# Weight loads of a hybrid decoder layer issued from ScalarE's DMA queue instead of SP's

## Chip, cores and metric

One Trainium2 chip, one NeuronCore of it. The metric is the device time of one execution in microseconds, the median of several runs. The kernel before takes 1884.48 us.

## The reference

One decoder layer on 2048 tokens and 16 meta tokens, model width 1024, all in float32. One input projection makes six groups of 1024 columns: q, k, v, a gate for the attention, the input and the gate of a linear recurrence (LRU). Eight heads of stick-breaking attention and eight blocks of a gated recurrence read the same normalised rows; both results are gated, normalised and go through one output projection.

```python
def hybrid_layer(h, ...):
    u = rmsnorm(h, pre_g)
    p = u @ w_in
    q, k, v, g_att, x_lru, g_lru = jnp.split(p, ...)
    att = rmsnorm(stick_breaking_attention(q, k, v), att_out_g) * jax.nn.silu(g_att)
    lru = rglru_branch(x_lru, conv_w, conv_b, gate_a_w, gate_a_b, gate_x_w, gate_x_b, lru_lambda)
    lru = rmsnorm(lru, lru_out_g) * jax.nn.silu(g_lru)
    y = jnp.concatenate([att, lru], axis=-1) @ w_out
    return h + rmsnorm(y, post_g)

def stick_breaking_attention(q, k, v):
    ...
        z = jnp.einsum('bhqd,bhkd->bhqk', qi, kh) * scale
        log_beta = jax.nn.log_sigmoid(z)
        log_1m = jnp.where(mask, log_beta - z, 0.0)
        suffix = lax.cumsum(log_1m, axis=3, reverse=True) - log_1m
        w = jnp.where(mask, jnp.exp(log_beta + suffix), 0.0)
        return jnp.einsum('bhqk,bhkd->bhqd', w, vh)
```

## The kernel before

Every product keeps float32 accuracy by splitting each operand into a high and a low half and multiplying three times (high-high, high-low, low-high).

**Projection.** The normalised rows lie in SBUF, transposed, as uH and uL. The 48 column blocks of w_in (128 columns each) are loaded one by one, 512 KB each, into a raw buffer (`wraw`, one of it; three of the first four go to spare rows and show as `lrow`). `load_w` is a generator: its first step issues the load (line 143), the next ones find the block's largest value (VectorE reduce at line 146, a small TensorE product at 152), scale it and split it into wH (ScalarE, line 161) and wL (VectorE, line 163). The end of wL frees the raw buffer. wH and wL have three buffers each; one comes free when the last chunk of its block has gone through TensorE (line 174, 24 matmuls a chunk). The chunk's result is evicted by ScalarE (line 792 for q and k, 841 for v, 888 for the gates, 341 for the LRU input).

**Attention.** For each head and 128 queries a segment of up to 1040 keys goes: scores on TensorE (line 219), sigmoid on ScalarE (223), a mask on GpSimd (228), a running product on VectorE (233), the split into two halves by ScalarE (245) and VectorE (251), a DMA transpose on the SP queue (256) that gives wT, and the product with v on TensorE (270). There are 208 segments.

**LRU.** For each of eight blocks the weights of its two gates (128 KB) are loaded by `lru_gates_w` (line 326) into one buffer `graw`; the next two lines split them into gH (ScalarE, 327) and gL (VectorE, 328). Behind that come a convolution (VectorE, lines 357 and 360), the gates' products (379, 380) and a recurrence (414).

**Order.** A planner (`Plan`, `weave`) runs when the program is built. It keeps an estimated free time for each engine, and emits an instruction when its inputs are ready by that estimate. For a load it reckons 0.6 us of SP and 4.5 us until the data are there (`LD`), at the start 0.5, 1.46 and 2.0 (`LDX`); `weight` emits the load and plans the reduce at that time. The order of TensorE, ScalarE and VectorE stays as emitted:

```python
    with tc.manual_schedule(engines={mybir.EngineType.PE, mybir.EngineType.Activation, mybir.EngineType.DVE}):
        start()
        weave()
```

The scheduler underneath orders SP and GpSimd itself, and may issue a load on SP as soon as its buffer is free. `weight` is called by `loader`, as soon as both a pair of wH/wL buffers and the raw buffer are free in the plan. `mix_start` calls `lru_gates_w` when a block's first half of LRU input is there, and reckons `LD` for it on ScalarE.

Of the kernel before, what the change touches and what calls it, by code (L numbers as in the profile page):

```python
# [70 lines left out]
def hybrid_layer(nc, tc, I, out):  # L71
    import contextlib
    act, dve, pool, pe, sp = nc.scalar, nc.vector, nc.gpsimd, nc.tensor, nc.sync
# [57 lines left out]
    def load_w(col, home=None, raw=None):  # L131


        if raw is None:
            raw = wp.tile([P, KT, P], F32, name="wraw", bufs=1)
        else:
            raw = raw[:, :D].rearrange("p (k c) -> p k c", k=KT)
        if home is None:
            wH = wp.tile([P, KT, P], F16, name="wH", bufs=3)
            wL = wp.tile([P, KT, P], F16, name="wL", bufs=3)  # L140
        else:
            wH, wL = (home.bitcast(F16)[:, x * D:(x + 1) * D].rearrange("p (k c) -> p k c", k=KT) for x in range(2))
        sp.dma_start(out=raw, in_=I["w_in"][col])
        yield
        m = sm.tile([P, 4], F32, name="wm", bufs=6)
        dve.tensor_reduce(out=m[:, 0:1], in_=raw, axis=AX.XY, op=ALU.max, apply_absolute_value=True)

        dg = sm.tile([P, P], BF16, name="dg", bufs=1)
        dve.tensor_scalar(out=dg, in0=identb, scalar1=m[:, 0:1], scalar2=None, op0=ALU.mult)
        yield  # L150
        ps = psm.tile([P, 512], F32, name="mm")
        pe.matmul(out=ps[:, :P], lhsT=onesb, rhs=dg, start=True, stop=True)
        yield
        dve.tensor_reduce(out=m[:, 1:2], in_=ps[:, :P], axis=AX.X, op=ALU.max)
        dve.tensor_scalar(out=m[:, 1:2], in0=m[:, 1:2], scalar1=1e-30, scalar2=2.0 ** -W_EXP, op0=ALU.max, op1=ALU.mult)
        dve.tensor_scalar(out=m[:, 1:2].bitcast(I32), in0=m[:, 1:2].bitcast(I32), scalar1=0x7F800000, scalar2=None,
                          op0=ALU.bitwise_and)
        dve.reciprocal(out=m[:, 3:4], in_=m[:, 1:2])
        dve.tensor_scalar(out=m[:, 2:3], in0=m[:, 1:2], scalar1=ius, scalar2=None, op0=ALU.mult)
        yield  # L160
        act.activation(out=wH, in_=raw, func=AF.Copy, scale=m[:, 3:4])
        yield
        dve.scalar_tensor_tensor(out=wL, in0=raw, scalar=m[:, 3:4], in1=wH, op0=ALU.mult, op1=ALU.subtract)  # L163
        yield
        yield wH, wL, m[:, 2:3]
# [154 lines left out]
    def lru_gates_w(c):  # L320


        raw = sl.tile([P, 2, P], F32, name="graw", bufs=1)
        gH = sl.tile([P, 2, P], F32R, name="gH", bufs=1)
        gL = sl.tile([P, 2, P], F32R, name="gL", bufs=1)
        sp.dma_start(out=raw, in_=I["gates"][c])
        act.copy(out=gH, in_=raw)
        dve.tensor_tensor(out=gL, in0=raw, in1=gH, op=ALU.subtract)
        return gH, gL
# [306 lines left out]
    def weight(home, raw, raw_done, prio=None):  # L636

        name = order[cursor[0]]
        cursor[0] += 1
        parts = load_w(ctile[name[:-1]] + int(name[-1]), home, raw)  # L640
        next(parts)
        J = lambda e, t, us, then: plan.job(e, prio, t, us, lambda: next(parts), then)
        t = (LD if prio is None else LDX)(plan.free["pe"])
        plan.at(t, lambda: J("dve", t, 1.45, lambda t: urgent.append((t + (3.0 if prio is None else 0.0), rmm, mm))))

        def mm():
            next(parts)
            J("dve", PE(0, 128), 1.2, lambda t: (rmm.put(t), J("act", t, 1.1, lambda t: J("dve", t, 1.25, end))))

        def end(t):  # L650
            loaded[name] = next(parts)
            ready[name] = t
            raw_done(t)
# [337 lines left out]
    def mix_start(c, m):  # L991
        hd = head[c]
        if "mix" not in hd:
            hd["mix"] = Mix(c, hd["xs"], lru_gates_w(c))
            A(LD(plan.free["pe"]), 256)
        elif m and hd["gates"] < 6:
            hd["conv1"] = lambda: mix_start(c, 1)
            return
        mix = hd["mix"]
        def conv_step(i):  # L1000
            mix.conv(m, [i])
            t = V(plan.free["pe"], HT)
            if i < 3:
                plan.at(t, lambda: conv_step(i + 1))
            else:
                plan.at(t, lambda: rrow.get(gates))

        def gates():
            t = plan.free["pe"]
            gate_in(c, m, 0, t)  # L1010
            gate_in(c, m, 1, t)
        conv_step(0)
# [509 lines left out]
```

## Time and profile before

| | |
|---|---|
| median of 3 runs | 1884.48 us (1883.80 to 1887.80) |
| profiled execution | 1882.98 us |
| its span, first to last instruction | 1881.1 us |
| granted TensorE clock, mean share | 0.989 |
| TensorE busy | 1795.0 us (95%) |
| VectorE busy | 1282.7 us (68%) |
| ScalarE busy | 1047.9 us (56%) |
| GpSimd busy | 343.3 us (18%) |
| DMA issues | all on SP's queue |

The span is one execution, taken by the profiler. In the rows, PE is TensorE, ACT ScalarE, DVE VectorE, SPq the queue of SP; L143 is line 143 of the kernel. A timeline row gives the start and the length in us, the engine, the line, the operation and what it writes and reads; in brackets stands how long the engine was idle before it and what ended that. Several like instructions in a row are one line with xcount, its length from the first start to the last end.

### The profile page before, as it was taken

Reading aid. Unit: us, or ns where it says so; the run is one execution under the profiler, and the core shown is the slowest. Engines: PE = TensorE matmul, PEld = TensorE weight load, DVE = VectorE, ACT = ScalarE, POOL = GpSimd, SP = SyncE. Lnnn points to the kernel's source line nnn. Section 1 sums busy time; section 2 is a strip of 40 time slices with the busy share of each in tenths; the row PEclk is TensorE's granted clock in tenths of the full one; section 3 lists DMA queues with packets and bytes.
Section 4 is the critical chain, followed back from the end, with each engine's and each line's share of the span. In section 5 each row is a group of like instructions: output and inputs, shape, how many; then the busy total and the mean of one; then the engine's idle time right before and its main releaser. Section 6 shows DMA issues by size and latency. Waiting matters only on the chain. (4 is left out here: it accounts for less than half of the span.)

```text
span 1881.1 us, 30861 instructions
## 1 busy us (share of the span) xinstructions
PE 1795.0 (95%) x12104; PEld 1155.2 (61%) x12104; DVE 1282.7 (68%) x1759; ACT 1047.9 (56%) x1789; POOL 343.3 (18%) x442
## 2 busy tenths in 40 slices
PE   3987999999999999998999899999999999999998
PEld 2544665566556655664665466556655678888776
DVE  8747876987778668767885788687857851134553
ACT  7768557556655755665567546665565742233221
POOL 0013012311320131014101401241131000002222
PEclk8998999999999999999999999999999999999999
DMA  6713650654175226433652355145405884354553
GB/s 211 144 29 74 125 109 27 123 105 87 49 139 104 63 54 127 97 64 65 134 100 55 73 126 98 46 97 132 83 30 108 192 184 144 96 177 154 179 190 134
DMA packets 428417, 203.46 MB, mean 108 GB/s; under 512 B 362976, under 2 KB 396768, under 8 KB 428272
## 3 DMA queue, kind: packets, MB, share of 16 engines
q1 hardware_dynamic: 428272, 201.49, 45.9%
q8 instruction: 95, 1.56, 0.3%
q14 instruction: 50, 0.41, 0.1%
HBM read 78.23 MB, written 34.08 MB: 60 GB/s over the span
## 5 line engine op out<-in xcount | busy, mean ns | idle before, releaser
L174 PE MATMUL mm<-uH,wH 128*128 128x512 f16 (+3 forms) x1808 | 616.3, 345 | 8.3 <-DVE sa L892 2.6
L174 PE MATMUL mm<-uL,wH 128*128 128x512 f16 (+3 forms) x1808 | 616.3, 345 | 0.0
L174 PE MATMUL mm<-uH,wL 128*128 128x512 f16 (+3 forms) x1808 | 615.4, 345 | 0.8 <-DVE wL L163 0.8
L174 PEld LDWEIGHTS <-wH 128*128 128x128 f16 x3616 | 333.9, 98 | 273.1 <-issue 10.4
L233 DVE TENSOR_TENSOR_SCAN row<-row 128x656 f32<-128x656 f32 (+6 forms) x208 | 352.4, 1695 | 131.9 <-POOL row L228 101.5
L174 PEld LDWEIGHTS <-wL 128*128 128x128 f16 x1808 | 177.3, 98 | 158.5 <-DVE wL L163 1.3
L270 PE MATMUL o<-wT,v 128*128 128x128 f16 x3392 | 224.4, 220 | 30.0 <-DMA wT<-w 26.5
L270 PEld LDWEIGHTS <-v 128*128 128x128 f16 x3392 | 206.1, 98 | 70.4 <-issue 27.0
L223 ACT ACTIVATE row<-z,zs 128x656 f32<-128x656 f32 (+6 forms) x208 | 171.5, 825 | 125.2 <-PE z L219 115.0
L251 DVE TENSOR_TENSOR w<-row,w 128x640 f16<-128x640 f32 (+5 forms) x208 | 179.8, 865 | 16.3 <-ACT w L245 14.4
L245 ACT CAST w<-row 128x640 f16<-128x640 f32 (+5 forms) x208 | 155.1, 746 | 51.8 <-DVE row L233 49.1
L537 PE MATMUL y<-woH,aH 128*128 128x512 f32 x352 | 140.8, 400 | 1.6 <-DVE w L251 1.6
L537 PE MATMUL y<-woH,aL 128*128 128x512 f32 x352 | 138.7, 394 | 0.5 <-DVE aL L530 0.5
L537 PE MATMUL y<-woL,aH 128*128 128x512 f32 x352 | 138.3, 393 | 0.6 <-DVE woL L490 0.6
L228 POOL TENSOR_SCALAR_AFFINE_SELECT row<-row 128x128 f32<-128x128 f32 x128 | 59.9, 469 | 406.4 <-ACT row L223 374.7
L219 PE MATMUL z<-kH,qH 128*128 128x328 f16 (+10 forms) x384 | 123.6, 322 | 0.6 <-ACT row L223 0.6
L219 PE MATMUL z<-kL,qH 128*128 128x328 f16 (+10 forms) x384 | 123.5, 322 | 0.0
L219 PE MATMUL z<-kH,qL 128*128 128x328 f16 (+10 forms) x384 | 123.4, 321 | 0.0
L219 PEld LDWEIGHTS <-qH 128*128 128x128 f16 x768 | 72.8, 98 | 56.3 <-issue 3.7
L369 DVE TENSOR_TENSOR cs<-lrow,cs 64x344 fp32r<-64x344 f32 x96 | 50.7, 528 | 78.5 <-ACT cs L368 71.3
L530 DVE TENSOR_TENSOR aL<-araw,aH 128x1024 fp32r<-128x1024 f32 x32 | 39.4, 1231 | 93.2 <-ACT aH L527 92.1
L1468 POOL TENSOR_TENSOR row<-row 128x512 f32<-128x512 f32 x32 | 46.5, 1454 | 262.9 <-ACT row L1467 251.1
(208 smaller groups left out, 2476.2 us busy)
## 6 DMA issues: line engine op xcount, KB each, us to landing
wraw<-in_w_in SPq DMA_DIRECT2D x45, 512.0 KB, 3.5
row<-in_x SPq DMA_DIRECT2D x22, 512.0 KB, 3.8
aa_d<-sa SPq DMA_DIRECT2D x34, 256.0 KB, 2.0
al_d<-sl SPq DMA_DIRECT2D x32, 256.0 KB, 2.4
araw<-in_w_out SPq DMA_DIRECT2D x16, 512.0 KB, 4.4
araw<-al_d SPq DMA_DIRECT2D x16, 512.0 KB, 4.3
yl_d<-ys SPq DMA_DIRECT2D x32, 256.0 KB, 2.1
row<-yl_d SPq DMA_DIRECT2D x16, 512.0 KB, 3.2
```

The lines of the kernel that those rows point to most:

```text
L174: pe.matmul(out=ps[:, :n], lhsT=a[:, kt, :], rhs=b[:, kt, c0:c0 + n], start=(k == 0), stop=(k == 3 * KT - 1))
L219: pe.matmul(out=z[:, a, :n], lhsT=l[:, qs], rhs=r[:, c], start=(x == 0), stop=(x == 2))
L223: act.activation(out=self.om[:, :L].rearrange("p (a c) -> p a c", a=self.parts), in_=self.z[:, :self.parts, :self.n], func=AF.Sigmoid, sca ...
L228: pool.affine_select(out=d, in_=d, pattern=[[-1, P]], compare_op=ALU.is_gt, fill=1.0, base=0, channel_multiplier=1)
L233: dve.tensor_tensor_scan(out=om, data0=om, data1=om, initial=self.pred.om[:, 0:1] if self.si else WS, op0=ALU.mult, op1=ALU.bypass)
L245: act.copy(out=w[:, r0:r0 + nb * P], in_=om[:, self.m0:self.L])
L251: dve.tensor_tensor(out=w[:, r0 + nb * P:r0 + 2 * nb * P], in0=om[:, self.m0:self.L], in1=w[:, r0:r0 + nb * P], op=ALU.subtract)
L270: pe.matmul(out=o[:, c], lhsT=l, rhs=r, start=(self.si == 0 and x == 0), stop=(self.last and x == len(prods) - 1))
L369: dve.tensor_tensor(out=cs[oth, :n], in0=xc[own, a:a + n], in1=cs[own, :n], op=ALU.subtract)
L530: dve.tensor_tensor(out=aL, in0=raw, in1=aH, op=ALU.subtract)
L537: pe.matmul(out=ps, lhsT=a[:, c, :], rhs=b[:, 512 * half:512 * half + 512], start=(c == 0 and x == 0), stop=(c == KT - 1 and x == 2))
L1468: pool.tensor_tensor(out=yt[:, cs], in0=yt[:, cs], in1=pg[:, cs], op=ALU.mult)
```

## The change

The load of a block of w_in and the load of a block's gate weights are issued by ScalarE instead of SP: 48 and 8 issues. Nothing else differs; the planner's reckoning of a load stays as it was.

```diff
@@ load_w
-        sp.dma_start(out=raw, in_=I["w_in"][col])
+        act.dma_start(out=raw, in_=I["w_in"][col])
         yield
@@ lru_gates_w
-        sp.dma_start(out=raw, in_=I["gates"][c])
+        act.dma_start(out=raw, in_=I["gates"][c])
         act.copy(out=gH, in_=raw)
         dve.tensor_tensor(out=gL, in0=raw, in1=gH, op=ALU.subtract)
```

## Rows read from the trace of the kernel before

**Rows 1.** Page, part 1: busy us, share of the span, instructions of each engine.

```profile
PE 1795.0 (95%) x12104; PEld 1155.2 (61%) x12104; DVE 1282.7 (68%) x1759; ACT 1047.9 (56%) x1789; POOL 343.3 (18%) x442
```

**Rows 2.** Stretches: start:end, length, busy us (instructions) by engine, clock, DMA share, GB/s.

```profile
0.00:94.00 94.00, 63.09 (x443) 40.27 (x444) 72.92 (x146) 70.21 (x116) 5.04 (x19) 0.91 0.70 178
94.00:188.00 94.00, 76.50 (x433) 40.73 (x431) 59.98 (x78) 71.90 (x108) 23.71 (x25) 0.93 0.25 51
```

**Rows 3.** Waits of TensorE, whole span: us in total, times, longest us.

```profile
PE o L270 <- DMA wT<-w: 26.5, 17, 5.1
```

**Rows 4.** Waits of the SP queue, whole span: us in total, times, longest us.

```profile
SPq L256 <- DVE w L251: 349.4, 147, 9.2
SPq L143 <- DVE wL L163: 204.6, 21, 17.9
```

**Rows 5.** Timeline of the SP queue: the start, around 142 us, around 212 us.

```profile
4.59 2.39 SPq L143 DMA_DIRECT2D lrow<-in_w_in  x3
...
141.92 0.34 SPq L143 DMA_DIRECT2D wraw<-in_w_in  x1
142.83 4.40 SPq L256 DMA_TRANSPOSE wT<-w  x2
...
211.50 0.88 SPq L143 DMA_DIRECT2D wraw<-in_w_in  x1
212.50 5.61 SPq L256 DMA_TRANSPOSE wT<-w  x2
```

**Rows 6.** Timeline of VectorE around 142 us and 212 us.

```profile
140.59 1.26 DVE L163 SCALAR_TENSOR_TENSOR wL<-wraw,wm,wH 128x1024 f16<-128x1024 f32 x1
...
142.53 0.28 DVE L251 TENSOR_TENSOR w<-row,w 128x128 f16<-128x128 f32 x1
...
211.06 0.95 DVE L251 TENSOR_TENSOR w<-row,w 128x768 f16<-128x768 f32 x1
```

**Rows 7.** Tile wraw: issues in ns (min/median/max), first and last start; landing in us.

```profile
L143 SPq DMA_DIRECT2D wraw<-in_w_in x45: 328/337/1062, 1.7 to 1392.0; - x45
...
DMA to landing us min/median/max: 3.0/3.5/6.0
```

**Rows 8.** Tile graw: durations in ns (min/median/max), first and last start; landing.

```profile
L326 SPq DMA_DIRECT2D graw<-in_gates x8: 338/770/1109, 7.1 to 1142.2; - x8
L327 ACT CAST gH<-graw x8: 387/396/402, 73.2 to 1320.4; 128x256 fp32r<-128x256 f32 x8
...
DMA to landing us min/median/max: 2.1/2.9/9.7
```

**Rows 9.** Timeline of ScalarE around 652 us and 673 us.

```profile
652.16 1.16 ACT L390 ACTIVATE row<-row,nsp 128x1032 f32<-128x1032 f32 x1
...
673.17 0.60 ACT L792 ACTIVATE qH<-mm 128x512 f16<-128x512 f32 x1 [3.63 <-PE mm L174]
```

**Rows 10.** Timeline of VectorE, 654 to 659 us.

```profile
654.63 1.21 DVE L146 TENSOR_REDUCE wm<-wraw 128x1 f32<-128x1024 f32 x1
...
658.10 0.56 DVE L796 SCALAR_TENSOR_TENSOR qL<-mm,qH 128x384 f16<-128x384 f32 x1 [1.96 <-ACT qH L792]
```

**Rows 11.** Timeline of VectorE behind two splits of gates, 775 and 595 us.

```profile
775.11 0.42 DVE L328 TENSOR_TENSOR gL<-graw,gH 128x256 fp32r<-128x256 f32 x1
...
784.21 1.06 DVE L369 TENSOR_TENSOR cs<-lrow,cs 64x344 fp32r<-64x344 f32 x2 [2.88 <-ACT cs L368]
...
613.17 0.51 DVE L369 TENSOR_TENSOR cs<-lrow,cs 64x344 fp32r<-64x344 f32 x1 [1.11 <-ACT cs L368]
...
616.07 0.96 DVE L251 TENSOR_TENSOR w<-row,w 128x768 f16<-128x768 f32 x1
```

**Rows 12.** Line 256 in 617.0 to 617.3 us: its one transpose's landing.

```profile
DMA to landing us min/median/max: 4.3/4.3/4.3
```

**Rows 13.** Timeline of TensorE, 620 to 624 us: the product that reads it.

```profile
623.15 1.05 PE L270 MATMUL o<-wT,v 128*128 128x128 f16 x16
```

**Rows 14.** Timeline of ScalarE, 0 to 11 us: its first compute.

```profile
7.07 1.06 ACT L690 ACTIVATE w<-acc_l 16x1024 f32<-16x1024 f32 x1 [5.06 <-DMA acc_l<-in_meta]
```

## The prediction, made before the change was run

> **What bounds the kernel now.** I read the busy table of the page first, then the busy time by stretch, then who waits for whom on TensorE and on the SP queue, and last the order of time around the loads. TensorE is busy 1795.0 us [rows 1] of a span of 1881.1 us, so all its idle time is 86.1 us, and no change of queues can win more than that. Over half of it lies in the first tenth: 94.00 - 63.09 = 30.9 us and 94.00 - 76.50 = 17.5 us [rows 2]. There VectorE and ScalarE are busy 72.92 and 70.21 us of the first 94, and TensorE waits for their normalised rows, not for a load. Behind 188 us some 38 us of idle are left. The largest item on the whole of TensorE's list is the transposed attention weights (wT), 26.5 us in 17 waits [rows 3]; they are made by DMA transposes that share the SP queue with the loads of the change. So the question is what those transposes wait for.
>
> **What the change removes.** The SP queue spends 204.6 us in 21 waits at line 143, for the free raw buffer (wL, line 163), and 349.4 us at line 256 for VectorE's split of the attention weights [rows 4]. The first number looks like a blocked queue. But a blocked queue costs only what stands ready behind it. The longest single wait of TensorE for wT, 5.1 us, is at 140.8: the load is issued at 141.92, when wL has ended (140.59 + 1.26 = 141.85), and the transpose behind it at 142.83 [rows 5], while its own input ends at 142.53 + 0.28 = 142.81 [rows 6]. The load cost it 0.02 us. I compared every transpose's issue with the end of its split: of 208, three stood behind an issue of line 143 or 326. The first: split ended at 211.06 + 0.95 = 212.01 [rows 6], load at 211.50 for 0.88, transpose at 212.50 [rows 5], so 0.49 us; the three together are 1.3 us, and part of it is slack. I take a gain of 0.3 us, between 0 and 1.3.
>
> **What it adds on ScalarE: issues.** ScalarE's order is written by hand, so each of 48 + 8 = 56 issues lies in it where the plan emits it. No row shows an issue on ScalarE. The nearest are the same loads on SP: 328 ns at least, 337 the median, 1062 the most [rows 7]; gates up to 1109 [rows 8]. So ScalarE gains 56 x 0.337 = 18.9 us of occupied time, at most 48 x 1.062 + 8 x 1.109 = 59.9. Most of it is free, because of the place. A weight's load is emitted when its buffer ring gets a slot back, that is when the last chunk of an older weight ends on TensorE, and ScalarE's next instruction in order is the eviction of that same chunk. At 673.17 ScalarE has stood idle 3.63 us for that eviction [rows 9]; the issue falls into this hole and even goes out before the hole ends. I take the median as the price and 0.4 us of the 18.9 as visible.
>
> The Trainium skill says (Perfetto Trace Analysis, DMA Instruction — HWDGE) that the descriptor generator is locked by one sequencer at a time, so an issue on ScalarE could wait for a transpose on SP. No run here shows a ScalarE issue; by that rule the price would lie nearer the 59.9 us than the 18.9. That bound is in the range below on its own grounds.
>
> **What it moves: the lead of the loads.** On SP a load goes out as soon as wL of the weight before has ended, often long before its use. In ScalarE's order it goes out at its emission, for which the plan (`LD` in line 625) reckons 5.1 us to the first use, the reduce at line 146. Landing takes 3.0 to 6.0, median 3.5 us [rows 7], so a load lands in time if ScalarE is less than 1.6 us behind. I went through 44 loads with the eviction as the place: some eight land late, by 1.0 to 2.4 us. The worst kind is the load emitted at 652.30: ScalarE is in tanh until 652.16 + 1.16 = 653.32 [rows 9], so the data come at 653.32 + 3.5 = 656.8 instead of ahead of the reduce at 654.63, 2.2 us late; VectorE then has a hole of 1.96 us at 658.10 [rows 10] that takes this up. TensorE's list of waits names no weight of that stretch. I take 0.4 us in all, between 0 and 6 (the late time of eight loads at half its size).
>
> **Gates.** Line 326 is followed at once by the copy of its data (line 327). On SP that load ran far ahead: the last one is issued at 1142.2 and copied at 1320.4 [rows 8]. Now ScalarE issues it and stands until it has landed: 2.1 to 9.7, median 2.9 us [rows 8], eight times, with VectorE's gL, the convolution and the scans queued behind. Two kinds of place: (a) at 775.11 VectorE's queue moves by 2.9 us, but it has a hole of 2.88 us at 784.21 [rows 11]: nothing is left, three places of this kind. (b) behind the copy near 595 VectorE has no hole until 613.17, and that one is 1.11 us, so the split at 616.07 is still 2.9 - 1.1 = 1.8 us late [rows 11]. It ends at 617.03 today, its transpose lands 4.3 us after an issue at 617.2 [rows 12], at 621.5, and TensorE takes it at 623.15 [rows 13]: 1.65 us of slack, so about 0.2 is lost, and a neighbour may lose as much or somewhat more, to 1 us. I take 0.5 at each of four such places and 0.1 at the other three: 2.3 us, between 0 and 7 x 2.9 = 20.3. The page's first gate load, near 73 us, is in the next part.
>
> **The first 190 us.** At the start ScalarE waits for its first rows until 7.07 anyway [rows 14], and four issues of 0.43 us fit behind its table load. But the last of the three loads issued at 4.59 took until 4.59 + 2.39 = 6.98 [rows 5], since each waits for an older transfer; if the table load of 1.28 us stands behind that issue in ScalarE's order, its first square starts at 8.26, 1.2 late. I take 0.7, from -0.5 (x loads move ahead by one issue) to 1.5. In the second stretch, with 17.5 us of idle on TensorE and 71.90 of ScalarE's 94 us taken [rows 2], two loads with their waits for wL stand in ScalarE's order, and a new weight is used as soon as it is ready; with the first gate load I take 1.0, from 0 to 4.
>
> **Sum**, against the profiled execution's own 1882.98 us: -0.3 + 0.4 + 0.4 + 2.3 + 0.7 + 1.0 = +4.5, that is 1887.5. The median of the runs, 1884.48, lies 1.5 above the profiled one, so I forecast 1889.0.
>
> **Rivals.** (1) The SP queue was the limit, faster: transposes also share the ring with 512 KB loads, and stores and transposes keep SP occupied. Then wT comes earlier by about an issue and part of a landing. It decides from the point where the 17 waits for wT [rows 3] follow a load on SP in time; one pair of them, near 518 us, does. Price: a fifth of 26.5 us, about -5.5, so 1879. The Trainium skill (Perfetto Trace Analysis, DMA Optimizations) says that balancing DMAs over issuing engines may help where descriptor generation is the limit; by that rule this rival wins, and the rows of the line-256 waits speak against its condition. Chance 0.10. (2) It doesn't do what it says: the scheduler, free to move SP's work, might also move ScalarE's issues early, ahead of the hand order; then the gates don't stall and 56 issues vanish in ScalarE's idle time: +-1.5, 1884.5. Line 1420 names ScalarE among the engines whose order stays as written, which speaks against it. Chance 0.15. (3) The gates' stalls and late loads go through to TensorE: 7 x 2.9 = 20.3 less the holes seen at three places (8.7), plus 3 for late loads: about +15, 1899. For it: the 17 waits for wT [rows 3] are places without any slack. Against it: they are 17 of 208, and the place of (b) has 1.65 us [rows 12, 13]. Chance 0.18.
>
> **How the numbers follow.** The forecast (+1 to +8) has 0.50, of which 0.20 below +3.8. Within 0.2% is 3.8 us, about what a measurement of this kernel can tell from no change. Rest 0.07, spread: a changed order on SP or GpSimd, which the scheduler writes itself. Faster 0.09 + 0.02 = 0.11; same 0.20 + 0.14 + 0.01 + 0.03 = 0.38; slower 0.30 + 0.01 + 0.18 + 0.02 = 0.51. The range runs from 1880 (rival 1 cut off in part) to 1899 (rival 3's middle).
>
> **What the profile after would show.** ScalarE issues at lines 143 and 326, each between the same neighbours as said; ScalarE idle about 2.9 us before each line 327; a wait of VectorE for wraw at line 146 of some 10 us in all, where it had almost none; the waits for wT near 26.5 us. If those fall by over 5 us, rival 1 holds; if line 326 stands far ahead of line 327, rival 2; if TensorE's idle time behind 188 us grows by over 10 us, rival 3.

## The result, and the profile after

The changed kernel takes 1904.11 us (median of four runs, 1901.22 to 1906.35), the kernel before 1885.21 us on the same chip: a ratio of 1.0096, with a 95% interval of 1.0081 to 1.0112, so some 18 us slower. The forecast was 1889.0 with 1899 as its upper end. The sign was right, the size about a quarter of what came, and the range missed.

The profiled execution of before (1882.98 us) is quicker than the medians of before in the comparisons below (1884.5 to 1886.9 us), so a trace laid over it can show some 2 to 4 us that do not belong to the edit, and differences of time below go by the ratios where two comparisons are set against each other. TensorE's granted clock, as a mean over the span, is 0.984 to 0.990 in the runs of before, and the lower values stand mostly with the longer times.

Page of the profile after, part 1, and the same two stretches as in [rows 2]:

```profile
PE 1809.5 (95%) x12104; PEld 1162.3 (61%) x12104; DVE 1284.0 (67%) x1759; ACT 1048.0 (55%) x1789; POOL 343.1 (18%) x442
```

```profile
0.00:94.00 94.00, 60.38 (x410) 38.86 (x411) 69.86 (x140) 63.94 (x105) 4.20 (x18) 0.91 0.65 166
94.00:188.00 94.00, 78.72 (x426) 41.44 (x424) 56.41 (x80) 75.17 (x116) 20.14 (x23) 0.91 0.24 56
```

TensorE does the same 12104 products, but is "busy" 14.5 us longer than in [rows 1] and idle only 94.8 - 86.1 = 8.7 us longer. The mean granted clock of this trace is 0.983, against 0.989 before: more of the same work ran at the lower of TensorE's two clocks (1.2 instead of 2.4 GHz), mostly behind some of its holes, as its idle stretches are called here. Whether this is a cost of its own is asked below.

Who waits for whom on TensorE, and on the SP queue (us in total, times, longest):

```profile
PE o L270 <- DMA wT<-w: 31.4, 17, 5.1
PE z L722 <- ACT w L697: 16.8, 4, 9.7
PE mm L379 <- DVE sa L892: 4.2, 5, 1.7
```

```profile
SPq L256 <- DVE w L251: 414.2, 153, 14.5
```

Line 143 is gone from SP's list, and SP's wait for VectorE at line 256 rose from 349.4 [rows 4] to 414.2. More of the freed time is at line 878, the transposes of v, whose waits together rose from 173.4 to 375.8 us. The freed time of SP became waiting for inputs. The waits for wT grew from 26.5 [rows 3] to 31.4 us. At line 722 the longest wait is that for the first normalised row, 9.7 us against 5.8. New on the list is a wait at line 379: TensorE stands before the gates' products for a VectorE instruction at line 892, which has nothing to do with the gates but frees the buffer that they need in PSUM, the memory into which TensorE writes its results.

The moved loads. Tile graw first, then tile wraw (issues in ns as min/median/max with first and last start; waits; landing in us):

```profile
L326 ACTq DMA_DIRECT2D graw<-in_gates x8: 334/335/344, 76.2 to 1341.3; - x8
...
  DMA graw<-in_gates: 20.6, 8
...
DMA to landing us min/median/max: 1.9/3.3/5.5
```

```profile
L143 ACTq DMA_DIRECT2D wraw<-in_w_in x45: 334/334/405, 0.7 to 1416.6; - x45
...
  DMA wraw<-in_w_in: 4.5, 2
...
DMA to landing us min/median/max: 3.0/3.5/5.3
```

An issue costs ScalarE 0.334 us, near the least value of [rows 7] and less than half the median of [rows 8]. The median landing is as before for wraw and 0.4 us longer for graw. All eight gate loads now stand directly ahead of their copy, and ScalarE idles 20.6 us there.

### The profile page after: what moved, and what is told of

Its sections match the earlier page's. It is cut to its first block, busy times and chain, and to the rows that moved or that the text cites. A ratio compares the mean times of both kernels' runs of the same rounds, so it can differ in the third digit from the quotient of the medians.

```text
span 1904.3 us, 30847 instructions
## 1 busy us (share of the span) xinstructions
PE 1809.5 (95%) x12104; PEld 1162.3 (61%) x12104; DVE 1284.0 (67%) x1759; ACT 1048.0 (55%) x1789; POOL 343.1 (18%) x442
## 5 line engine op out<-in xcount | busy, mean ns | idle before, releaser
L270 PE MATMUL o<-wT,v 128*128 128x128 f16 x3392 | 228.0, 222 | 31.5 <-DMA wT<-w 31.4
L251 DVE TENSOR_TENSOR w<-row,w 128x640 f16<-128x640 f32 (+5 forms) x208 | 183.9, 885 | 17.2 <-ACT w L245 16.4
L243 ACT CAST w<-row 128x32 f16<-128x32 f32 x128 | 27.4, 214 | 127.1 <-DVE row L233 117.9
```

Source lines behind the costliest of these rows:

```text
L243: act.copy(out=mv[:, :, 0:NM], in_=om[:, 0:NM].unsqueeze(1).broadcast_to([P, 2, NM]))
L251: dve.tensor_tensor(out=w[:, r0 + nb * P:r0 + 2 * nb * P], in0=om[:, self.m0:self.L], in1=w[:, r0:r0 + nb * P], op=ALU.subtract)
L270: pe.matmul(out=o[:, c], lhsT=l, rhs=r, start=(self.si == 0 and x == 0), stop=(self.last and x == len(prods) - 1))
```

## Experiments

First the change is split, then single terms are taken away. The diffs show the lines that matter; where others are left out stands `...`.

**Gates alone.**

```diff
-        sp.dma_start(out=raw, in_=I["gates"][c])
+        act.dma_start(out=raw, in_=I["gates"][c])
```

> Only the eight gate loads (line 326) go to ScalarE; the 48 projection loads stay on SP. Theory A (the stalls at the gates carry the loss: ScalarE stands before line 327 until the data land, the PSUM buffers that it and VectorE should have freed come late, and TensorE waits at lines 174 and 379): the trace of the change shows 3.3 us at the first gate load and 1.65 + 2.8 + 1.9 = 6.4 us at three later ones, so before plus 9.7, about 1895 us (+8 to +12), with VectorE's sa and cs as TensorE's releasers at line 379. Theory B (the projection loads in ScalarE's order carry it): before plus 1 to 3, 1886.5 to 1888 us, and TensorE's list without the sa entries.

Measured: 1899.38 us, ratio 1.0071 [1.0058, 1.0083], +13.4 us. Theory A holds in kind, with a size somewhat above its range of 8 to 12. The order of GpSimd's and of SP's other instructions is that of before.

**Projection loads alone.**

```diff
-        sp.dma_start(out=raw, in_=I["w_in"][col])
+        act.dma_start(out=raw, in_=I["w_in"][col])
```

> Only the 48 projection loads (line 143) go to ScalarE; the gate loads stay on SP. Theory A: what is left is the start (3.1 us later by 36 us) and the longer holes of TensorE at four head starts with the half clock behind them, before plus 9, about 1894 us (+6 to +11). Theory B: before plus 16 to 18, about 1902 us. If the half clock at the head starts needs the gate stalls ahead of it, before plus 3 to 4.

Measured: 1895.74 us, ratio 1.0052 [1.0040, 1.0064], +9.8 us. This is theory A's size, though the next run takes the start out of its account. Neither half is free. Together they would give 23 us, so some 5 us of the two overlap.

**Start on SP.**

```diff
...
-        parts = load_w(ctile[name[:-1]] + int(name[-1]), home, raw)
+        parts = load_w(ctile[name[:-1]] + int(name[-1]), home, raw, act if prio is None else sp)
```

> As the change, but the four weight loads of the start stay on SP. If the start's 3.1 us (two queues fetch together, and ScalarE's order at the start is changed) last to the end: 3 us less than the change, about 1901 us, with the first normalised row as early as before (14.3 us against 15.9). If the shift is taken up by later holes: the change's own time within 0.5 us, 1904 us.

Measured: 1905.42 us, ratio 1.0109 [1.0093, 1.0124], against 1.0096 for the change. The first normalised row is at TensorE at 14.03 us instead of 15.86, and nothing of the 3 us shows at the end. The start is no term of the loss that these times can tell. Why the first row came late is seen in the change, on ScalarE:

```profile
2.70 1.28 ACT L690 ACT_TABLE_LOAD   x1 [2.70 <-issue]
8.68 1.06 ACT L690 ACTIVATE w<-acc_l 16x1024 f32<-16x1024 f32 x1 [4.69 <-DMA acc_l<-in_meta]
```

The table load behind the four issues ends at 3.98 us and holds up nothing; the first square waits until 8.68 for its rows, which land 1.6 us later than in [rows 14].

**Gates ahead.** The load of block c + 1 is issued by ScalarE behind the last gate of block c; the first stays where it was.

```diff
...
+                if head[c]["gates"] == 12 and c + 1 < H:
+                    graw[c + 1] = graw_load(c + 1)
```

> As the change, but the gate loads of blocks 1 to 7 are issued by ScalarE a block ahead, behind the last gate of the block before, so that only the first of the eight copies at line 327 waits for its data. Theory A: ScalarE's wait there falls from 20.6 us to about 3, the waits of line 379 for sa go, and the time falls by 6.4 us (5 to 10) to about 1898 us. Theory B: within 1.5 us of the change, 1904 us, though the wait falls all the same.

Measured: 1898.99 us, ratio 1.0070 [1.0057, 1.0083], 4.9 us below the change, at the lower end of what theory A gave. ScalarE's wait falls from 20.6 to 5.8 us, all of it at the first copy. The steps at TensorE's gates go: against the trace of the change it gains 1.65 us at 621 us, 1.0 and 2.0 at 988 and 992, 1.1 at 1362. Theory A holds.

How a stall of ScalarE reaches TensorE is seen in the change at the gate load of 600 us. ScalarE, VectorE and TensorE (start, us, what, idle time before and its releaser):

```profile
600.72 0.34 ACTq L326 DMA_DIRECT2D graw<-in_gates  x1
604.04 0.40 ACT L327 CAST gH<-graw 128x256 fp32r<-128x256 f32 x1 [2.21 <-DMA graw<-in_gates]
```

```profile
604.48 0.43 DVE L328 TENSOR_TENSOR gL<-graw,gH 128x256 fp32r<-128x256 f32 x1 [4.09 <-ACT gH L327]
...
620.17 0.75 DVE L892 SCALAR_TENSOR_TENSOR sa<-mm,us,sa 128x512 f32<-128x512 f32 x1
```

```profile
620.98 0.43 PE L379 MATMUL mm<-cs,gH 128*128 128x344 f32 x1 [1.17 <-DVE sa L892]
```

Behind the copy VectorE stands 4.09 us (1.76 us at the same place in before, line 328), then works without a pause, and 16 us later its eviction at line 892 ends so late (620.17 + 0.75 = 620.92) that TensorE has no free buffer until 620.98. The same eviction and the same product in before:

```profile
611.31 0.75 DVE L892 SCALAR_TENSOR_TENSOR sa<-mm,us,sa 128x512 f32<-128x512 f32 x1
```

```profile
613.01 0.44 PE L379 MATMUL mm<-cs,gH 128*128 128x344 f32 x1
```

There the eviction ends at 612.06, 0.95 us before the product, which doesn't wait. VectorE's further delay of 4.09 - 1.76 = 2.33 us takes up these 0.95 us of slack and leaves 1.4; TensorE's wait is 1.17.

**The issues alone.** All loads stay on SP; ScalarE issues 56 tiny loads at the same places.

```diff
-        sp.dma_start(out=raw, in_=I["w_in"][col])
+        sp.dma_start(out=raw, in_=I["w_in"][col]); act.dma_start(out=sm.tile([P, 4], F32, name="dum", bufs=2), in_=I["pp"][:, 0:4])
...
```

> The kernel before, with all its loads on SP, and 56 small extra loads (16 bytes a partition, nobody reads them) issued by ScalarE at the places of lines 143 and 326. It prices the issues alone. Theory C (as in the prediction): about 56 x 0.334 = 18.7 us more of ScalarE's time, hidden almost wholly, before plus 0.4 and at most 1 us. Rival: at the head starts ScalarE's casts stand on the chain to the transposes, so the issues pass to TensorE: before plus 5 to 8 us, with longer waits for wT there.

```profile
L143 ACTq DMA_DIRECT2D dum<-in_pp x48: 334/334/459, 0.7 to 1397.5; - x48
```

Measured: 1887.17 us, ratio 1.0002 [0.9993, 1.0010], +0.3 us. Theory C holds: 18.7 us of issues are hidden.

**A fill of GpSimd behind the masks.** Laying the orders of GpSimd side by side shows the next term: in the change, with the projection loads moved, four of its instructions stand elsewhere; with only the gate loads moved none does. GpSimd's order is the scheduler's, not the hand's. Of the four places one shows plainly in TensorE's waits, head 6: a fill of 80 columns (line 241, zeros for padding) that waits for a transpose to land is now ahead of a mask (line 228), where before it was behind. GpSimd, before and then after:

```profile
1242.79 1.04 POOL L850 TENSOR_TENSOR row<-row 128x512 f32<-128x512 f32 x1
1243.78 1.51 POOL L228 TENSOR_SCALAR_AFFINE_SELECT row<-row 128x128 f32<-128x128 f32 x1
1249.52 0.16 POOL L241 MEMSET w<- 128x80 f16 x1 [4.22 <-DMA wT<-w]
```

```profile
1258.49 1.04 POOL L850 TENSOR_TENSOR row<-row 128x512 f32<-128x512 f32 x1
1265.16 0.17 POOL L241 MEMSET w<- 128x80 f16 x1 [5.62 <-DMA wT<-w]
1265.28 0.29 POOL L228 TENSOR_SCALAR_AFFINE_SELECT row<-row 128x128 f32<-128x128 f32 x1
```

The mask starts right behind the product of line 850 in before, and 5.8 us after it in the change. VectorE's scan and TensorE's output follow late (VectorE and TensorE, after):

```profile
1265.61 1.79 DVE L233 TENSOR_TENSOR_SCAN row<-row 128x784 f32<-128x784 f32 x1 [3.88 <-POOL row L228]
```

```profile
1272.48 1.89 PE L270 MATMUL o<-wT,v 128*128 128x128 f16 x16 [3.29 <-DMA wT<-w]
```

```diff
-                pool.memset(w[:, 3 * NM:P], 0.0)
+                pool.tensor_scalar(out=w[:, 3 * NM:P], in0=om[:, 0:P - 3 * NM], scalar1=0.0, scalar2=None, op0=ALU.mult) if (self.h, self.i) == (6, 6) else pool.memset(w[:, 3 * NM:P], 0.0)
```

> As the change, but one small fill of GpSimd (line 241 for head 6, query tile 6) is made from that tile's own weights, so that it can't stand ahead of the masks of tiles 5 and 6 in GpSimd's order, where the scheduler put it once line 143 had left SP. Theory D (GpSimd's changed order: the mask stands behind a fill that waits for a transpose to land, and scan, split, transpose and TensorE follow): the hole of 3.3 to 3.6 us at the output of head 6, tile 4, goes, and the time falls by 3 to 5 us against the change, to about 1900 us. Rival (the hole comes from the loads, the changed order only goes with it): the hole stays, 1904 us within 1.

Measured: 1899.43 us, ratio 1.0077 [1.0065, 1.0090], 3.6 us below the change by the ratios, 4.7 by the medians. The two were compared in different sets and their intervals overlap, so the time alone doesn't show it; the trace does. The mask runs at 1260.14 again and the hole shrinks from 3.29 to 0.85 us:

```profile
1270.75 1.07 PE L270 MATMUL o<-wT,v 128*128 128x128 f16 x16 [0.85 <-DMA wT<-w]
```

Theory D holds for this hole, and its price is confirmed by the runs with late fills below.

**Holes filled.** The trace of the change has more time at the lower of TensorE's two clocks than the trace of before, mostly behind holes where a head starts. Idle products of TensorE in these holes ask whether that is a loss of its own.

```diff
+            for x in range((20 if self.i == 3 else 8) if self.si == 0 and 2 <= self.h <= 6 and self.i in (3, 4) else 0): pe.matmul(out=o[:, c if self.i == 3 else slice(0, 512)], lhsT=kqv["qH"][:, 0:P], rhs=kqv["kH"][:, 0:128 if self.i == 3 else 512], start=True, stop=True)
             for x, (l, r) in enumerate(prods): pe.matmul(out=o[:, c], lhsT=l, rhs=r, start=(self.si == 0 and x == 0),
```

> As the change, but ahead of the outputs of tiles 3 and 4 in heads 2 to 6, where TensorE waits for wT, TensorE does idle matrix products (20 of 128 columns or 8 of 512) into the bank that the output then starts anew: work in a hole, with nothing else changed. Theory E (10 to 13 us of the loss are time at half clock behind these holes): the granted clock stays at 1.00 behind them and the time falls by 6 us (4 to 10), to about 1898 us. Rival (the holes themselves are the loss, or the clock falls all the same): 1904 to 1907 us, for the products that don't fit into the holes.

Measured: 1903.85 us, ratio 1.0096 [1.0082, 1.0110]: no change. Two of the places, the change first and then the filled one (columns as in [rows 2]; the granted clock is the number behind POOL):

```profile
710.00:717.00 7.00, 5.14 (x25) 2.68 (x24) 4.74 (x8) 3.03 (x8) 1.38 (x4) 0.76 0.47 122
...
1086.00:1093.00 7.00, 4.00 (x22) 2.59 (x23) 6.69 (x8) 4.60 (x11) 5.34 (x4) 0.58 1.08 182
```

```profile
707.00:714.00 7.00, 5.65 (x50) 3.45 (x49) 3.71 (x6) 1.96 (x6) 0.41 (x2) 1.00 0.41 88
...
1086.00:1093.00 7.00, 7.00 (x63) 4.51 (x62) 6.67 (x9) 4.69 (x10) 3.10 (x4) 1.00 1.04 142
```

The clock stayed at 1.00 at three of five places, fell at the other two, and no time came back. But the run isn't clean: in heads 3 to 6 the idle products of tile 4 had to wait for their PSUM bank, a new wait of TensorE:

```profile
PE o L269 <- ACT ot L282: 10.1, 4, 2.8
```

What the clock gave back may have been lost in these 10.1 us, so the run doesn't price the half clock. Two other runs speak against theory E as an account of the loss. The trace with the issues alone has a mean granted clock of 0.984, near the 0.983 of the change, and its time is that of before. And the pair of runs with late fills below has the same clock in both traces, 0.989, and the change still costs its 14 us there.

**Gate stall doubled.**

```diff
-        sp.dma_start(out=raw, in_=I["gates"][c])
+        for _ in range(2): act.dma_start(out=raw, in_=I["gates"][c])
```

> As the run with only the gates on ScalarE, but each gate load is issued twice, the second behind the landing of the first, so that ScalarE stands about 3.2 us longer before line 327, eight times. Theory A (the stalls are the loss of the gates): 9 to 20 us more than with one load each, 1908 to 1919 us, with longer waits at lines 174 and 379 in the same places and at places that had none. Rival (the gates' loss is half clock and chance at the head starts): within 3 us of it, 1897 to 1902 us.

Measured: 1915.15 us, ratio 1.0149 [1.0136, 1.0163]; 14.7 us more than one load each. ScalarE's wait for graw and TensorE's for VectorE at line 379, with one load and with two:

```profile
ACT gH L327 <- DMA graw<-in_gates: 18.8, 8, 4.2
...
PE mm L379 <- DVE cs L369: 4.1, 3, 2.0
PE mm L379 <- DVE sa L892: 3.7, 3, 1.7
```

```profile
ACT gH L327 <- DMA graw<-in_gates: 40.5, 8, 6.5
...
PE mm L379 <- DVE cs L369: 10.2, 6, 2.9
```

21.7 us more of stall make 14.7 us more of time: 0.68. The first 18.8 us cost 13.4: 0.71. By the intervals each share is good to about 0.15. So on the mean some 0.7 of each microsecond of stall reaches the end, in both steps.

**Fills late, before and change.** In the trace of before such fills stand ahead of the masks in heads 3, 4, 5 and 7. GpSimd in head 5:

```profile
1068.00 0.17 POOL L241 MEMSET w<- 128x80 f16 x1 [5.64 <-DMA wT<-w]
1068.12 0.29 POOL L228 TENSOR_SCALAR_AFFINE_SELECT row<-row 128x128 f32<-128x128 f32 x1
```

Both runs use the edit of the fill above for `self.i == 6 and self.h > 2`.

> The kernel before, all loads on SP, but GpSimd's small fill (line 241) of query tile 6 in heads 3 to 7 is made from that tile's own weights, as in the run with the fill of head 6 alone, so that no mask of tile 5 or 6 stands behind a fill that waits for a transpose to land. In the trace of before such a fill stands ahead of the mask in heads 3, 4, 5 and 7 (waits of 5.63, 5.58, 5.64 and 3.29 us on GpSimd), in head 6 it does not. Theory D (this order costs TensorE a hole per head): the holes at the outputs of tile 4 in heads 3 to 5 (1.7, 2.8 and 3.4 us) shrink below 1 us and the time falls by 6 to 12 us below before, about 1877 us. Rival (the holes come from the transposes of v beside them): within 2 us of before.

> As the change, with the fills of tile 6 in heads 3 to 7 made late as in the run on the kernel before. It asks what the change costs where GpSimd's order plays no part. If gates (9 us by the steps of TensorE's order), start and landing are what is left: 9 to 11 us above the run on before with late fills. If the change costs its 13 to 14 us there too, something in the projection loads' place costs 4 us that no run has named.

Measured: before with late fills 1875.08 us, ratio 0.9952 [0.9938, 0.9965], 9 us faster than before; the holes at tile 4 of heads 3 to 5 are all under 0.5 us. The change with late fills 1889.29 us, ratio 1.0027 [1.0016, 1.0038]. The change costs 14.2 us between these two. Both traces have a mean granted clock of 0.989, so they can be laid over each other: the change is 4.6 us behind when the first gate is through (1.9 of it are made up by 229 us) and loses 6.0 at the gates of three later blocks, those whose copies run at 602, 967 and 1328 us. The other 5.4 us are what is left of some 7 us lost at the starts of heads 3 to 6, at tiles 3 and 4; the rest of the 7 is made up elsewhere. Two places of GpSimd's order besides the fills still differ between the two (lines 424 and 850), and one fill of head 5.

**Gates ahead and one fill.** The edits of the two runs above together, with the first gate load at the start.

> As the change, but all eight gate loads are issued ahead by ScalarE (the first at the start, the others behind the last gate of the block before), and the one fill of head 6, tile 6 stands behind the masks. If the terms are separate: the change less 5 (gates ahead) less 4.7 (fill) less 2.9 (first gate), about 1891 us, before plus 4 to 5; with the issues at 0.3 what is left over then belongs to the place of the projection loads. If the terms overlap: 1894 to 1897 us.

Measured: 1891.09 us, ratio 1.0037 [1.0024, 1.0050], +7.0 us over before. The time is the 1891 us expected if the terms are separate; against the before of its own comparison, what is left is more than the 4 to 5 us expected.

**The load beside the transposes.** What is left is at the head starts. The SP queue of before with late fills in head 3, then SP, ScalarE and TensorE of the change with late fills at the same place:

```profile
700.17 0.58 SPq L143 DMA_DIRECT2D wraw<-in_w_in  x1
703.30 1.30 SPq L256 DMA_TRANSPOSE wT<-w  x1
704.69 1.23 SPq L878 DMA_TRANSPOSE v<-sv  x1
706.10 1.37 SPq L256 DMA_TRANSPOSE wT<-w  x1
```

```profile
707.20 1.27 SPq L878 DMA_TRANSPOSE v<-sv  x1
708.65 1.26 SPq L256 DMA_TRANSPOSE wT<-w  x1
```

```profile
707.60 0.34 ACTq L143 DMA_DIRECT2D wraw<-in_w_in  x1
```

```profile
714.53 1.07 PE L270 MATMUL o<-wT,v 128*128 128x128 f16 x16 [1.92 <-DMA wT<-w]
```

SP sends the load 3.1 us ahead of a transpose; it is all but down when the transposes of the next tiles come. ScalarE sends it 1.05 us ahead of the transpose on which TensorE will wait. Landing of that one transpose (line 256), before and change, both with late fills:

```profile
DMA to landing us min/median/max: 3.5/3.5/3.5
```

```profile
DMA to landing us min/median/max: 5.8/5.8/5.8
```

The same happens in heads 4, 5 and 6 (5.7 to 6.2 us). In heads 1 and 2, whose loads the runs below move as well, the load itself landed in 4.1 and 4.2 us, so there the effect is smaller.

It happens from SP's own queue as well. In before with late fills four transposes stand 1.0 to 1.1 us behind a load that SP itself issued (at 401, 588, 946 and 1302 us); they land in 5.2 to 5.5 us. In the change with late fills the loads go out elsewhere, and the same four transposes land in 3.8 to 4.2. The second of them, before and change:

```profile
DMA to landing us min/median/max: 5.4/5.4/5.4
```

```profile
DMA to landing us min/median/max: 4.2/4.2/4.2
```

Three runs test what it costs; the edit of the first is

```diff
...
-        parts = load_w(ctile[name[:-1]] + int(name[-1]), home, raw)
+        parts = load_w(ctile[name[:-1]] + int(name[-1]), home, raw, sp if cursor[0] > 12 and cursor[0] % 6 == 1 else act)
```

The second does the reverse on the kernel before with late fills. The third adds gate loads issued ahead to the first, which is the run that its text calls the one before it.

> As the change with late fills, but six of the 48 projection loads stay on SP: in heads 1 to 6 the one that falls beside the transposes of v and of the first query tiles (line 143, issued at 344, 529, 708, 888, 1072 and 1252 us in the run with late fills). There it landed in 5.5 to 6.0 us instead of 3.5, and the transpose of wT behind it in 5.7 to 6.2 us instead of 3.3 to 3.5. Theory F (where ScalarE issues it, this load runs beside the transposes on which TensorE waits; SP issues it between them): 5 us (3 to 7) less than the change with late fills, about 1884.5 us, with the holes at tile 4 of heads 3 and 6 gone. Rival (the slow transposes have slack or the loss is elsewhere in the 48): within 1.5 us of it, 1888 to 1891 us.

> The kernel before with late fills, and only those six projection loads on ScalarE. Theory F: 5 us (3 to 7) more than without, about 1880 us, with slower transposes of wT beside these loads (over 4 us instead of 3.3) and a hole at tile 4 in some of heads 3 to 6. Rival: 1874 to 1876.5 us.

> As the run before this one, with all eight gate loads issued ahead by ScalarE as well. All terms named so far are then off: the gates' stalls, GpSimd's order, the load beside the transposes. If that is the whole account: within 3 us of the kernel before with late fills, 1875 to 1878 us, though 42 projection loads and 8 gate loads go out on ScalarE. If something is left: 1880 us or more.

Measured, in one comparison: the change with late fills and six loads back on SP 1883.90 us, 0.9994 [0.9984, 1.0003], 6.2 us below the run without that by the ratios, with the holes at tile 4 of heads 3 and 6 (1.92 and 0.99 us) gone; those six loads alone on ScalarE 1881.46 us, 0.9973 [0.9963, 0.9983], 4.0 us above before with late fills; all terms off 1872.58 us, 0.9933 [0.9921, 0.9944], below the 1875 to 1878 expected and the lowest median of the runs here, with 42 projection loads and 8 gate loads on ScalarE. Theory F holds on both sides, with the runs that it is set against in another comparison. In the second run the transposes beside the six loads land in 5.5 to 6.3 us in heads 3 to 6, and TensorE has holes of 1.5 to 2.2 us at tile 4 of these heads, where before with late fills has none. The longest, in head 5:

```profile
1073.08 1.51 PE L270 MATMUL o<-wT,v 128*128 128x128 f16 x16 [2.16 <-DMA wT<-w]
```

The page of the third run, and its longest group of waits:

```profile
PE 1797.5 (96%) x12104; PEld 1158.1 (62%) x12104; DVE 1282.7 (69%) x1759; ACT 1048.4 (56%) x1789; POOL 349.6 (19%) x442
```

```profile
PE o L270 <- DMA wT<-w: 18.3, 12, 5.4
```

## Why the prediction was right and wrong

The account, by differences of ratios times 1885 us: the change costs 0.0096 = 18.1 us. GpSimd's order: late fills win 0.0069 in the change and 0.0048 in before, so 0.0021 = 4.0 us belong to the change. The six loads beside the transposes: 1.0027 - 0.9994 = 0.0033 = 6.2 us. The gates' stalls: 0.9994 - 0.9933 = 0.0061 = 11.5 us. What remains, everything else about the move, is 0.9933 - 0.9952 = -0.0019 = -3.6 us, a small gain if anything: the two kernels were compared in different sets and their intervals overlap. By the intervals each of these differences is good to some 3 to 4 us. So the gates and the six loads are clear of noise as times; GpSimd's part rests on its holes in the traces and on the 9 us of the late fills. The split also depends on the order in which terms are taken away: the six loads were priced with the fills late, and in the change itself the transposes behind them land in 4.1 to 5.1 us, not 5.7 to 6.2.

**What bounds the kernel: right.** TensorE, with wT as its largest item. SP's 204.6 us of waiting at line 143 went without a gain clear of noise, and the freed time became waiting at lines 256 and 878.

**What it removes (-0.3): not contradicted.** The remaining -3.6 us may hold more of a relief than 0.3. The Trainium skill (Perfetto Trace Analysis, DMA Optimizations) says that balancing DMAs over issuing engines may help if descriptor generation is the bottleneck; that this is such a gain is not shown.

**Issues on ScalarE (+0.4): right.** 0.3 us (-1.3 to 1.9 by the interval), at 0.334 each. The Trainium skill (Perfetto Trace Analysis, DMA Instruction — HWDGE) has the descriptor generator locked by one sequencer at a time; no issue of wraw on ScalarE took over 405 ns, beside transposes that SP issues in 1.1 to 4.2 us. The one at 707.60 above took 0.34 us inside SP's issue of 1.27 us at 707.20.

**The lead of the loads (+0.4): wrong in kind.** VectorE's late reduces came out small, 4.5 us of waiting for wraw in two places against the 10 expected. But the step asked only when the data are needed, not what is on the DMA rings when they travel. The load that moves in time meets other transfers: 6.2 us, the second largest term, which the sum put at nothing. Rival 1 even had the rings with the opposite sign, as a relief for the transposes.

**Gates (+2.3, bounds 0 to 20.3): the mechanism right, the term mis-sized.** The stall was 20.6 us for all eight loads, 15.3 of it at the seven whose bound was 20.3, and 0.56 (11.5 us) to 0.71 of it reached the end, not 0.1. The sum had 2.3 for seven loads and the first in another line, so 11.5 stands against at most 3.3. The sorting into two kinds held: in the traces with late fills nothing is lost at the place of (a) near 775 [rows 11] nor at the two like it. The step that failed is the price of kind (b), a walk along one chain: from the stall to the late split to the transpose to wT, where 1.65 us of slack lie [rows 12, 13] and 0.2 were to be lost. At that very place TensorE was held at line 379 instead, by the eviction at line 892 in the same delayed queue, a path with 0.95 us of slack, and three of the four places of this kind lost 1.4 to 3.0 us each, where the sum had 0.5. Some 2 to 3 us more are lost at the first gate. Where the rest of the 11.5 us goes stays open. Bound every consumer of the stalled engines' queue, not the nearest.

**The first 190 us (+1.7): right in direction, no term at the end.** The first row came 1.5 us later than before, by late rows and not by the table load as the prediction had it, and with the start on SP the time stayed. The first gate cost 2 to 3 us in the traces; it is in the gates' term.

**A changed order on GpSimd (in the rest of 0.07): under-weighted.** It cost 4.0 us by the account above. The prediction named it and gave it no price, although the trace of before has the price: masks late by a fill's wait of 5.6 us in heads 3, 4 and 5.

**Rivals.** Rival 3 (stalls and late loads go through) was the nearest in size and cause, at 0.18; its sign in the profile, idle time behind 188 us growing by over 10 us, came out at 45.9 - 37.7 = 8.2 us; the other 14.5 us of the longer span show as busy time of TensorE, at a lower mean clock. Rival 1 and rival 2 fell: lines 143 and 326 stand in ScalarE's order where they were emitted.

## What to carry to other kernels

When a load moved to a compute engine's queue here, its issue was cheap; three other things were not. A consumer directly behind it makes that engine stand for the landing, and everything else in that engine's queue and behind it, the eviction of a PSUM buffer above all, goes with it, so issue the load one stage ahead. The load also travels at another time, beside other transfers, and the engines whose order the scheduler writes get another order: lay the orders of both programs side by side, and look at what is in flight when the load goes out.

## What the runs showed of the hardware that was not expected

- Beside a 512 KB load that starts about 1 us ahead of it, a DMA transpose of attention weights landed after 5.7 to 6.2 us instead of 3.5 in heads 3 to 6 with late fills (4.1 to 5.1 in the change itself), and the load itself after 5.5 to 6.0 instead of 3.5. It happened from either queue: 5.2 to 5.5 us behind loads of SP's own, against 3.8 to 4.2 for the same transposes without them. The small transpose of 128 columns at 143.9 us, 0.9 us behind a load, landed in 2.9 all the same.
- Behind holes of TensorE of 1 to 4 us the granted clock fell to 0.50 (1.2 GHz) for 3 to 7 us in some places and not in others, such as 1.00 behind the hole of 3.45 us at 1075 us in before. Over the whole span the mean granted clock of before is 0.984 to 0.990 from one execution to the next. With idle products in the holes it stayed at 1.00 in three of five places, in a run whose time did not change.
- A fill of 0.16 us on GpSimd that waits 5.6 us for a transpose, ahead of a mask, goes with a hole of TensorE of 1.8 to 3.5 us in each of heads 3, 4 and 5 of before. With the fills of heads 3 to 7 late these holes are gone and the kernel is 9 us faster.
